# Moving split weights by 64 bytes in an encoder whose matmuls read them from SBUF

## The chip, the cores and the metric

The kernel runs on one core of one Trainium2 chip. The metric is the device time of one execution in microseconds (us); lower is better. All weights and activations are float32. TensorE multiplies in the reduced type float32r, and to keep more of the precision each operand is split into a high part ("hi", rounded to float32r) and a low part ("lo", the remainder).

## The reference

The reference is a two-layer encoder trunk on 256 tokens of width 2048. Layer 0 mixes tokens with a gated width-3 convolution, layer 1 with dilated banded attention (16 heads, three groups of dilation 1, 4 and 16). Each is followed by a gated feed-forward block of inner width 5632 with a width-3 convolution.

```
for i in range(2):
    h = rmsnorm(x, mix_norm_g[i])
    x = x + (short_conv_mixer if i == 0 else dilated_attention_mixer)(h, ...)
    h = rmsnorm(x, ffn_norm_g[i])
    x = x + conv_ffn(h, w_up[i], conv_w[i], conv_b[i], w_down[i])
return rmsnorm(x, final_norm_g)

short_conv_mixer: u, b, c = split(h @ w_in);  (b * dwconv3(c * u)) @ w_out
conv_ffn:         a, b = split(dwconv3(h @ w_up));  (silu(a) * b) @ w_down
attention:        softmax over |i-j| <= half within each dilation, groups joined by
                  their softmax denominators, then @ w_out
```

Nearly all the work is in the products with the weight matrices. All of them are read once from HBM.

## The kernel before

Activations lie transposed: 128 channels on the partitions, 16 blocks of channels, and for each block 256 tokens of hi followed by 256 tokens of lo (tiles `h`, `y`, `a`, `o`). A product with a 128x128 weight block takes two matmuls. The hi weights are loaded into TensorE, and 512 columns (hi and lo activations) stream past; then the lo weights are loaded, and the 256 columns of hi activations stream past. The product lo times lo is left out. Both add into one PSUM tile `ps`, whose halves are added on the way out (`gathered`: a ScalarE copy of one half, a VectorE addition of the other). Below, a "pair" is such a 512-column and 256-column matmul, and the load that runs during a stream is that of the next matmul.

Weights come through `load_w`: SyncE issues a DMA of up to 16 blocks into `raw` (four buffers), ScalarE rounds eight blocks at a time into the hi half of a `w2` tile, and VectorE subtracts to make the lo half. The four `w2` tiles are 8448 bytes per partition each, 33 times 256, and begin at multiples of 256 bytes. The hi blocks begin there; the lo blocks begin 4096 + 64 bytes further (`OFF = 16` words), so 64 bytes past a multiple of 256. Each block is 512 bytes wide, so this holds for every block. The activations `h`, `y`, `a`, `o` all begin at multiples of 256.

Four places use other forms. The first 16 blocks of each of the first three products come through `w2s`, whose hi and lo parts both begin at multiples of 256 (lines 205 to 210). The v projections of the attention (`v_unit`) swap the operands: blocks of `h` are the weights, all at multiples of 256, and a `w2v` tile (the `w2` buffers again) streams, beginning 64 bytes past a multiple; there the code issues eight 512-column matmuls, then eight 256-column ones. The last down-projection (`last`) uses three 256-column matmuls for each block, so that one VectorE addition ends a block. Scores, transposes and the product of probabilities and v are small and run between the q and k projections as tasks.

The order of instructions on each engine is set by the framework's scheduler out of the order of the code. In `mm` the code has eight hi matmuls, then eight lo matmuls of the same `w2` tile; the program that comes out of it alternates between them, 512 and 256 columns, wherever `mm` is used. The number of weight pairs that pass through `mm` (lines 108 and 110) is 6816; the v units have 768 (lines 374 and 377); the last down-projection has 176 blocks (lines 250 to 252).

Of the kernel before, what the change touches and what calls it, by code (L numbers as in the profile page):

```python
# [31 lines left out]
OFF = 16  # L32
W2 = 2 * 8 * P + 64
QSCALE = float(P) ** -0.5
# [3 lines left out]
def encoder_kernel(ctx: ExitStack, tc: tile.TileContext, xT, gs, scw, fcw, dist, w_first, w_in, w_so, w_v, w_qk, w_ao, w_up, w_dn, out):  # L38
# [42 lines left out]
    def load_w(src, n):  # L81
# [11 lines left out]
    def mm1(ps, w, a, start, stop):  # L93
        pe.matmul(ps, w[:, 0, :], a, start=start, stop=False)  # L94
        return pe.matmul(ps[:, :T], w[:, 1, :], a[:, :T], start=False, stop=stop)  # L95

    def mm(ps, parts, a, ks):


        n = len(parts)  # L100
        ks = list(ks)
        while ks:
            w2 = parts[ks[0]][0]
            now = [k for k in ks if parts[k][0] is w2]
            hi, lo = w2
            ks = ks[len(now) :]
            for k in now:
                pe.matmul(ps, hi[:, parts[k][1], :], a[:, k, :], start=k == 0, stop=False)  # L108
            for k in now:
                ins = pe.matmul(ps[:, :T], lo[:, parts[k][1], :], a[:, k, :T], start=False, stop=k == n - 1)  # L110
        return ins
# [66 lines left out]
    def add_to_x(ps, j):  # L178
        e = gathered(ps, "e0")
        dve.tensor_add(x[:, j, :], x[:, j, :], e)  # L180


    def short_conv():
        with tc.tile_pool(name="sc", bufs=1) as sp:
# [13 lines left out]
            for n in (1, 1, 2, 2, 3, 3, 2, 1, 1):  # L198
# [6 lines left out]
                w2 = sp.tile([P, 2, 3, 3 * P], F32R, name="w2s", tag="w2s", bufs=2)  # L205
                ins = split(w2[:, 0, :n, :], w2[:, 1, :n, :], raw[:, :n, :])
                for part in range(3):
                    for k in range(k0, k0 + n):
                        w = w2[:, :, k - k0, part * P : (part + 1) * P]
# [35 lines left out]
    def last(ps, parts, a, j):  # L245

        xj = x[:, j, :]
        for k in range(CH):
            (hi, lo), i = parts[k]
            pe.matmul(ps[:, :T], hi[:, i, :], a[:, k, T:], start=k == 0, stop=False)  # L250
            pe.matmul(ps[:, :T], lo[:, i, :], a[:, k, :T], start=False, stop=False)  # L251
            pe.matmul(ps[:, :T], hi[:, i, :], a[:, k, :T], start=False, stop=k == CH - 1)  # L252
        dve.tensor_add(xj, xj, ps[:, :T])
# [83 lines left out]
    def attention():  # L337
        with tc.tile_pool(name="att", bufs=1) as sp:
# [18 lines left out]
            def v_unit(hp, g):  # L357
# [239 lines left out]
```

## Time and profile before

| what | value |
|---|---|
| median of 3 runs | 2802.68 us (2802.38 to 2804.01) |
| profiled execution, its own time | 2801.87 us |
| its span, first to last instruction | 2800.1 us |
| granted TensorE clock, mean | 0.999 |
| PE (matmul) busy | 2783.2 us, 99% |
| PEld (weight load) busy | 2470.5 us, 88% |
| DVE (VectorE) busy | 1992.8 us, 71% |
| ACT (ScalarE) busy | 1504.0 us, 54% |
| HBM | 185 GB/s over the span |

The busy time of a matmul in the profile includes its way through the pipeline, so that consecutive ones overlap: the 512-column matmuls show 393 ns each and the 256-column ones 280 ns, though one follows the other sooner. What a matmul costs is the distance from its start to the next start. It is read from the timeline, from the pieces of the chain of waits (which are cut at the next start), or from the number of matmuls in a long stretch.

### The profile page before, as it was taken

Reading aid. Unit: us, or ns where it says so; the run is one execution under the profiler, and the core shown is the slowest. Engines: PE = TensorE matmul, PEld = TensorE weight load, DVE = VectorE, ACT = ScalarE, POOL = GpSimd, SP = SyncE. Lnnn points to the kernel's source line nnn. Section 1 sums busy time; section 2 is a strip of 40 time slices with the busy share of each in tenths; the row PEclk is TensorE's granted clock in tenths of the full one; section 3 lists DMA queues with packets and bytes.
Section 4 is the critical chain, followed back from the end, with each engine's and each line's share of the span. In section 5 each row is a group of like instructions: output and inputs, shape, how many; then the busy total and the mean of one; then the engine's idle time right before and its main releaser. Section 6 shows DMA issues by size and latency. Waiting matters only on the chain.

```text
span 2800.1 us, 40840 instructions
## 1 busy us (share of the span) xinstructions
PE 2783.2 (99%) x16388; PEld 2470.5 (88%) x16388; DVE 1992.8 (71%) x3065; ACT 1504.0 (54%) x2320; POOL 0.7 (0%) x6
## 2 busy tenths in 40 slices
PE   9999999999999999999999999999999999999998
PEld 7888888888888888888888888888888888888888
DVE  8777788876867768665665666666778876877865
ACT  6444566555655556544444444444565655555554
POOL 0000000000000000000000000000000000000000
PEclk9999999999999999999999999999999999999999
DMA  7555555546555456545445455455455546555553
GB/s 256 202 183 194 193 185 195 186 167 217 184 168 214 168 188 220 185 173 177 173 177 177 169 182 176 171 179 181 167 194 187 189 168 211 193 167 211 176 185 135
DMA packets 79822, 519.50 MB, mean 186 GB/s; under 512 B 9104, under 2 KB 10256, under 8 KB 28816
## 3 DMA queue, kind: packets, MB, share of 16 engines
q1 hardware_dynamic: 79488, 516.37, 52.4%
q8 instruction: 128, 2.10, 0.3%
q14 instruction: 62, 0.51, 0.1%
q10 hardware_dynamic: 144, 0.52, 0.0%
HBM read 514.76 MB, written 2.10 MB: 185 GB/s over the span
## 4 chain that ended last, share of the span: by engine, by line
PE 99%; DVE 0%; DMA 0%; SPq 0%; ACT 0%; issue 0%; DVEq 0%; ACTq 0%
PE ps L108 56%; PE ps L110 29%; PE ps L374 6%; PE ps L377 3%; PE ps L251 1%; PE ps L250 1%; PE ps L252 1%; PE ot L465 1%; PE s L423 1%; PE pt L442 1%; PE ot L460 0%; PE ps L94 0%; DMA raw<-in_w_first 0%; PE ps L95 0%; DVE x L284 0%; PE s L411 0%
## 5 line engine op out<-in xcount | busy, mean ns | idle before, releaser
L108 PE MATMUL ps<-h,w 128*128 128x512 f32 x5072 | 1769.0, 393 | 0.0
L110 PE MATMUL ps<-h,w 128*128 128x256 f32 x5072 | 1417.8, 280 | 0.0
L77 DVE TENSOR_TENSOR w<-raw,w 128x1024 fp32r<-128x1024 f32 (+1 forms) x954 | 1081.5, 1134 | 381.0 <-ACT w L76 362.2
L76 ACT CAST w<-raw 128x1024 fp32r<-128x1024 f32 (+1 forms) x954 | 934.0, 979 | 540.8 <-PE ps L110 423.8
L108 PEld LDWEIGHTS ps<-h,w 128*128 128x128 f32 x5072 | 952.2, 188 | 201.4
L110 PEld LDWEIGHTS ps<-h,w 128*128 128x128 f32 x5072 | 962.8, 190 | 0.5 <-DVE w L77 0.4
L120 ACT COPY tmp<-ps 128x256 f32<-128x256 f32 x464 | 172.3, 372 | 486.8 <-PE ps L110 486.8
L108 PE MATMUL ps<-a,w 128*128 128x512 f32 x1232 | 427.4, 392 | 0.0
L122 DVE TENSOR_TENSOR e<-ps,tmp 128x256 f32<-128x256 f32 x464 | 195.8, 422 | 243.9 <-ACT tmp L120 243.9
L110 PE MATMUL ps<-a,w 128*128 128x256 f32 x1232 | 344.3, 280 | 0.0
L108 PEld LDWEIGHTS ps<-a,w 128*128 128x128 f32 x1232 | 231.2, 188 | 49.4
L110 PEld LDWEIGHTS ps<-a,w 128*128 128x128 f32 x1232 | 233.9, 190 | 0.0
L374 PE MATMUL ps<-w2v,h 128*128 128x512 f32 x768 | 193.5, 394 | 0.0
L77 DVE TENSOR_TENSOR w2v<-rawv,w2v 128x1024 fp32r<-128x1024 f32 x96 | 117.6, 1225 | 98.1 <-ACT w2v L76 96.7
L374 PEld LDWEIGHTS ps<-w2v,h 128*128 128x128 f32 x768 | 137.6, 188 | 24.4
L76 ACT CAST w2v<-rawv 128x1024 fp32r<-128x1024 f32 x96 | 100.6, 1047 | 96.1 <-PE ps L377 69.4
L134 ACT ACTIVATE cv<-e,fcw_sb 128x256 f32<-128x256 f32 x176 | 105.8, 602 | 12.5 <-DVE e L129 11.9
L377 PEld LDWEIGHTS ps<-w2v,h 128*128 128x128 f32 x768 | 103.0, 188 | 8.0
L377 PE MATMUL ps<-w2v,h 128*128 128x256 f32 x768 | 105.0, 278 | 0.0
L129 DVE TENSOR_TENSOR e<-e,rr 128x256 f32<-128x256 f32 x220 | 93.0, 424 | 6.8
L135 DVE SCALAR_TENSOR_TENSOR cv<-e,fcw_sb,cv 128x255 f32<-128x255 f32 x176 | 84.1, 479 | 8.0 <-ACT cv L134 8.0
L136 DVE SCALAR_TENSOR_TENSOR cv<-e,fcw_sb,cv 128x255 f32<-128x255 f32 x176 | 85.1, 485 | 6.1
(120 smaller groups left out, 1711.6 us busy)
## 6 DMA issues: line engine op xcount, KB each, us to landing
raw<-in_w_up SPq DMA_DIRECT2D x176, 1024.0 KB, 4.8
raw<-in_w_qk SPq DMA_DIRECT2D x96, 1024.0 KB, 4.7
raw<-in_w_dn SPq DMA_DIRECT2D x128, 704.0 KB, 4.0
rawv<-in_w_v SPq DMA_DIRECT2D x48, 1024.0 KB, 5.0
raw<-in_w_in SPq DMA_DIRECT2D x45, 1024.0 KB, 4.8
raw<-in_w_so SPq DMA_DIRECT2D x16, 1024.0 KB, 4.8
raw<-in_w_ao SPq DMA_DIRECT2D x16, 1024.0 KB, 4.8
raw<-in_w_first SPq DMA_DIRECT2D x3, 384.0 KB, 5.6
```

Of the source, the lines that this page charges most:

```text
L76: ins = act.copy(hi, src)
L77: dve.tensor_sub(lo, src, f32(hi))
L108: pe.matmul(ps, hi[:, parts[k][1], :], a[:, k, :], start=k == 0, stop=False)
L110: ins = pe.matmul(ps[:, :T], lo[:, parts[k][1], :], a[:, k, :T], start=False, stop=k == n - 1)
L120: act.copy(tmp, ps[:, T:])
L122: dve.tensor_add(e, ps[:, :T], tmp)
L129: dve.tensor_mul(e, g, r)
L134: act.activation(c, e, AF.Identity, bias=w[:, 3:4], scale=w[:, 1:2])
L135: dve.scalar_tensor_tensor(c[:, 1:], e[:, : T - 1], w[:, 0:1], c[:, 1:], op0=ALU.mult, op1=ALU.add)
L136: dve.scalar_tensor_tensor(c[:, : T - 1], e[:, 1:], w[:, 2:3], c[:, : T - 1], op0=ALU.mult, op1=ALU.add)
L374: pe.matmul(ps[i], h[:, k, i * P : (i + 1) * P], w2[:, k - k1, :, :], start=k == 0, stop=False)
L377: pe.matmul(ps[i][:, :T], h[:, k, T + i * P : T + (i + 1) * P], w2[:, k - k1, 0, :], start=False, stop=k == KT - 1,)
```

## The change

Offsets are given in words of 4 bytes. In the `w2` tiles the hi blocks now begin at word 16 (64 bytes past a multiple of 256) and the lo blocks at word 1088 (a multiple of 256); the same is done to `w2s`. For the v units the `w2v` tile is laid out as four lo blocks from word 0 and four hi blocks from word 1040 (64 bytes past a multiple), and the 512-column stream takes the lo block first and then the hi block, by a stride. The 256-column stream is the hi block. The v units, `mm` and all but the last block row of the last down-projection (15 of 16) are written as 512 and 256 columns in turn; in the last down-projection these 15 now use `mm` and `add_to_x`, which is a ScalarE copy and two VectorE additions in place of one VectorE addition.

```diff
-OFF = 16
 W2 = 2 * 8 * P + 64
+HI = 16
+LO = 8 * P + 64
+LOV = 0
+LOS = 9 * P + 64
+HIV = 4 * 2 * P + 16
...
-            hi, lo = (w2[:, z : z + 8 * P].rearrange("p (k c) -> p k c", k=8) for z in (0, 8 * P + OFF))
+            hi, lo = (w2[:, z : z + 8 * P].rearrange("p (k c) -> p k c", k=8) for z in (HI, LO))
...
     def mm(ps, parts, a, ks):
         n = len(parts)
-        ks = list(ks)
-        while ks:
-            w2 = parts[ks[0]][0]
-            now = [k for k in ks if parts[k][0] is w2]
-            hi, lo = w2
-            ks = ks[len(now) :]
-            for k in now:
-                pe.matmul(ps, hi[:, parts[k][1], :], a[:, k, :], start=k == 0, stop=False)
-            for k in now:
-                ins = pe.matmul(ps[:, :T], lo[:, parts[k][1], :], a[:, k, :T], start=False, stop=k == n - 1)
+        for k in ks:
+            (hi, lo), i = parts[k]
+            pe.matmul(ps, hi[:, i, :], a[:, k, :], start=k == 0, stop=False)
+            ins = pe.matmul(ps[:, :T], lo[:, i, :], a[:, k, :T], start=False, stop=k == n - 1)
         return ins
...
-                w2 = sp.tile([P, 2, 3, 3 * P], F32R, name="w2s", tag="w2s", bufs=2)
-                ins = split(w2[:, 0, :n, :], w2[:, 1, :n, :], raw[:, :n, :])
+                w2 = sp.tile([P, LOS + 9 * P], F32R, name="w2s", tag="w2s", bufs=2)
+                w2 = [w2[:, z : z + 9 * P].rearrange("p (k c) -> p k c", k=3) for z in (HI, LOS)]
+                ins = split(w2[0][:, :n, :], w2[1][:, :n, :], raw[:, :n, :])
...
     def last(ps, parts, a, j):
-        for k in range(CH):
-            (hi, lo), i = parts[k]
-            pe.matmul(ps[:, :T], hi[:, i, :], a[:, k, T:], start=k == 0, stop=False)
-            pe.matmul(ps[:, :T], lo[:, i, :], a[:, k, :T], start=False, stop=False)
-            pe.matmul(ps[:, :T], hi[:, i, :], a[:, k, :T], start=False, stop=k == CH - 1)
-        dve.tensor_add(xj, xj, ps[:, :T])
+        if j < KT - 1:
+            mm(ps, parts, a, range(CH))
+            add_to_x(ps, j)
+        else:
...
-                        w2 = w2[:, OFF : OFF + 8 * T].rearrange("p (k z c) -> p k z c", k=4, z=2)
-                        split(w2[:, :, 0, :], w2[:, :, 1, :], raw[:, k1 - k0 : k1 - k0 + 4, :])
+                        lo, hi = (w2[:, z : z + 4 * T].rearrange("p (k c) -> p k c", k=4) for z in (LOV, HIV))
+                        split(hi, lo, raw[:, k1 - k0 : k1 - k0 + 4, :])
+                        both = w2[:, : 2 * HIV].rearrange("p (z c) -> p z c", z=2)
                         for k in range(k1, k1 + 4):
+                            c = (k - k1) * T
                             for i in range(2):
-                                pe.matmul(ps[i], h[:, k, i * P : (i + 1) * P], w2[:, k - k1, :, :], start=k == 0, stop=False)
-                        for k in range(k1, k1 + 4):
-                            for i in range(2):
+                                pe.matmul(ps[i], h[:, k, i * P : (i + 1) * P], both[:, :, c : c + T], start=k == 0, stop=False)
                                 pe.matmul(
-                                    ps[i][:, :T], h[:, k, T + i * P : T + (i + 1) * P], w2[:, k - k1, 0, :],
+                                    ps[i][:, T:], h[:, k, T + i * P : T + (i + 1) * P], hi[:, k - k1, :],
                                     start=False, stop=k == KT - 1,
                                 )
```

Where `mm` was used before, TensorE's order stays as it was. It changes in two places. The first is the entry into the attention's v units on TensorE; the rows name the line, the operation, the tile written and those read, and the columns that stream. Before:

```order
L108 MATMUL ps<-a,w_10305 128x512
L110 MATMUL ps<-a,w_10305 128x256
L374 MATMUL ps<-w2v,h 128x512 x8
L377 MATMUL ps<-w2v,h 128x256 x8
L374 MATMUL ps<-w2v,h 128x512 x8
```

After:

```order
L108 MATMUL ps<-a,w_10305 128x512
L109 MATMUL ps<-a,w_10305 128x256
L380 MATMUL ps<-w2v,h 128x512
L381 MATMUL ps<-w2v,h 128x256
L380 MATMUL ps<-w2v,h 128x512
```

The same matmuls in number and size, now one of 512 columns, one of 256.

The second place is the last down-projection, here one block row on ScalarE (L76 and L81 make hi weights, L153 and L152 square the sum, L256 and L260 multiply by the norm's gain). Before:

```order
L76 CAST w_25763<-raw 128x1024
L76 CAST w_25766<-raw 128x384
L153 ACTIVATE sq<-x 128x256
L256 ACTIVATE x<-x,g_sb 128x256
L76 CAST w_25810<-raw 128x1024
```

After:

```order
L119 COPY tmp<-ps 128x256
L81 CAST w_25766<-raw 128x384
L152 ACTIVATE sq<-x 128x256
L81 CAST w_25806<-raw 128x1024
L260 ACTIVATE x<-x,g_sb 128x256
```

One copy out of PSUM is added for each block row. On TensorE each of these 15 block rows has 22 matmuls (11 pairs) where it had 33 of 256 columns; the last block row keeps its 33, and with it the end of the program is as it was.

More of the change, by code (lines that the diff above doesn't have):

```diff
@@ L247, in last @@
         xj = x[:, j, :]
-        for k in range(CH):
-            (hi, lo), i = parts[k]
-            pe.matmul(ps[:, :T], hi[:, i, :], a[:, k, T:], start=k == 0, stop=False)
-            pe.matmul(ps[:, :T], lo[:, i, :], a[:, k, :T], start=False, stop=False)
-            pe.matmul(ps[:, :T], hi[:, i, :], a[:, k, :T], start=False, stop=k == CH - 1)
-        dve.tensor_add(xj, xj, ps[:, :T])
+        if j < KT - 1:
+            mm(ps, parts, a, range(CH))
+            add_to_x(ps, j)
+        else:
+            for k in range(CH):
+                (hi, lo), i = parts[k]
+                pe.matmul(ps[:, :T], hi[:, i, :], a[:, k, T:], start=k == 0, stop=False)
+                pe.matmul(ps[:, :T], lo[:, i, :], a[:, k, :T], start=False, stop=False)
+                pe.matmul(ps[:, :T], hi[:, i, :], a[:, k, :T], start=False, stop=k == CH - 1)
+            dve.tensor_add(xj, xj, ps[:, :T])
         if j < KT - 1:
@@ L384, in v_unit @@
                     tmp = tp.tile([P, T], F32, name="tmp", tag="tmp")
-                    act.mul(tmp, ps[i][:, T:], rc[:, i : i + 1])
+                    act.mul(tmp, ps[i][:, :T], rc[:, i : i + 1])
                     e = tp.tile([P, T], F32, name="e", tag="e0") if g == 0 else v[:, i, :]
-                    dve.scalar_tensor_tensor(e, ps[i][:, :T], rc[:, i : i + 1], tmp, op0=ALU.mult, op1=ALU.add)
+                    dve.scalar_tensor_tensor(e, ps[i][:, T:], rc[:, i : i + 1], tmp, op0=ALU.mult, op1=ALU.add)
                     if g == 0:
```

6 lines of the change are left out of this document (3 added, 3 removed).

## The prediction

> **What bounds the kernel now.** I read the page first: engines, slices, chain, groups.
>
> ```profile
> PE 2783.2 (99%) x16388; PEld 2470.5 (88%) x16388; DVE 1992.8 (71%) x3065; ACT 1504.0 (54%) x2320; POOL 0.7 (0%) x6
> PEclk9999999999999999999999999999999999999999
> PE 99%; DVE 0%; DMA 0%; SPq 0%; ACT 0%; issue 0%; DVEq 0%; ACTq 0%
> L108 PE MATMUL ps<-h,w 128*128 128x512 f32 x5072 | 1769.0, 393 | 0.0
> L110 PE MATMUL ps<-h,w 128*128 128x256 f32 x5072 | 1417.8, 280 | 0.0
> ```
>
> TensorE sets the time from start to end: it is 99% of the chain, its matmuls wait for nothing (the last column is 0.0 idle), and the granted clock is at the top in all slices. So only the distance between matmuls counts. The count of matmuls in a stretch gives it, and the timeline gives its two parts.
>
> ```profile
> 300.00:800.00 500.00, 499.80 (x1442) 270.52 (x1441) 1.00 0.53 186
> ...
> 1200.40 0.28 PE L110 MATMUL ps<-h,w 128*128 128x256 f32 x1
> 1200.40 0.19 PEld L108 LDWEIGHTS ps<-h,w 128*128 128x128 f32 x1
> 1200.51 0.39 PE L108 MATMUL ps<-h,w 128*128 128x512 f32 x1
> 1200.52 0.19 PEld L110 LDWEIGHTS ps<-h,w 128*128 128x128 f32 x1
> 1200.74 0.28 PE L110 MATMUL ps<-h,w 128*128 128x256 f32 x1
> ```
>
> The first row is line 108 alone: 1442 matmuls in 500 us, so a pair takes 500 / 1442 = 346.7 ns. In the timeline the 512-column stream takes 0.23 us (1200.51 to 1200.74), and the 256-column one the rest, about 117 ns. Each load begins with the stream before its own. So during a 512-column stream the lo weights are read (64 past a multiple, the stream itself at a multiple), and during a 256-column stream the hi weights (both at a multiple). 6816 pairs at 346.7 ns are 2363 us of the 2800.
>
> **Does the address matter at all?** The v units answer best, in the chain of waits, whose pieces (start, length, what) end at the next start:
>
> ```profile
> 1323.81 1.84 PE ps L374 x8
> 1325.65 0.94 PE ps L377 x8
> 1326.60 1.83 PE ps L374 x8
> 1328.43 0.91 PE ps L377 x8
> 1329.34 1.83 PE ps L374 x8
> 1331.17 0.94 PE ps L377 x8
> 1332.11 1.83 PE ps L374 x8
> 1333.94 0.91 PE ps L377 x8
> 1334.85 0.44 PE s L423 x4
> ```
>
> Here all streams begin 64 past a multiple and all loads at one. The 512-column stream takes 1.83 / 8 = 228.8 ns. The 256-column stream has two steady lengths, 0.94 / 8 = 117.5 and 0.91 / 8 = 113.8 ns, with the same instructions and addresses; each holds for a run of eight. From 1323.81 to 1334.85 are 32 pairs, so 345.0 ns a pair. The startup has a third arrangement, everything at a multiple, and alternates like the main loop:
>
> ```profile
> 22.48 0.23 PE ps L94
> 22.71 0.12 PE ps L95
> 22.83 0.23 PE ps L94
> 23.06 0.11 PE ps L95
> 23.17 0.23 PE ps L94
> ...
> 25.25 0.23 PE ps L94
> 25.49 0.12 PE ps L95
> 25.60 0.23 PE ps L108
> ```
>
> Nine pairs from 22.48 to 25.60 are 3.12 us, 346.7 ns each; the 256-column streams take 0.11 and 0.12 in turn, about 115, which leaves 231.7 ns for the 512-column ones. The last down-projection has 256-column streams alone, all at a multiple; the loads during L251 and L252 are at a multiple, that during L250 (the lo weights of L251) 64 past one:
>
> ```profile
> 2753.06 0.28 PE L250 MATMUL ps<-a,w 128*128 128x256 f32 x1
> 2753.17 0.28 PE L251 MATMUL ps<-a,w 128*128 128x256 f32 x1
> 2753.29 0.28 PE L252 MATMUL ps<-a,w 128*128 128x256 f32 x1
> ...
> 2755.18 0.28 PE L250 MATMUL ps<-a,w 128*128 128x256 f32 x1
> ...
> L250 PEld LDWEIGHTS ps<-a,w 128*128 128x128 f32 x176 | 33.1, 188 | 0.0
> L251 PEld LDWEIGHTS ps<-a,w 128*128 128x128 f32 x176 | 33.8, 192 | 0.0
> ```
>
> Six blocks from 2753.06 to 2755.18 are 2.12 us, 353.3 ns for three, 117.8 each. The load at 64 past takes 192 ns instead of 188, and its stream is no longer than the others. So stream and load do act on each other, by a few ns, and the same pair of addresses can settle at more than one length.
>
> **The change part by part.** *Addresses in the main loop.* Afterwards the lo weights, at a multiple like the stream, are read during the 512-column stream, and the hi weights, 64 away from the stream, during the 256-column one. For the 256-column stream the nearest rows with a difference of 64 are the v units' (113.8 or 117.5) and L250's (117.8). For the 512-column stream with no difference there is the startup alone (231.7); with a difference, 228.8 in the v units. Bounds of the pair: at best 228.8 + 112 (a little below 113.8, as the startup's 0.11 allows) = 340.8; at worst 231.7 + 117.8 = 349.5. I take the v units' short length for the 256-column stream, because a difference of 64 is what separates them from the main loop, which stays at 117, and for the 512-column stream the middle of its two rows, 230.3. That makes 344.1 ns, 2.6 less than 346.7, times 6816: 17.7 us less.
>
> *v units.* 768 pairs go from 345.0 to 344.1 if they behave as the main loop does: 0.7 us less. With bounds of 340.8 and 349.5 it is 3.2 less to 3.5 more.
>
> *Last down-projection.* 15 x 11 = 165 blocks go from 353.3 to 344.1: 1.5 us less (bounds 2.1 and 0.6 less). What it adds is cheap:
>
> ```profile
> L120 ACT COPY tmp<-ps 128x256 f32<-128x256 f32 x464 | 172.3, 372 | 486.8 <-PE ps L110 486.8
> L122 DVE TENSOR_TENSOR e<-ps,tmp 128x256 f32<-128x256 f32 x464 | 195.8, 422 | 243.9 <-ACT tmp L120 243.9
> ```
>
> 372 ns on ScalarE and another 422 ns on VectorE for each block row lie beside some 3.8 us of TensorE work (11 pairs at 344). Uncovered they would cost 15 x 0.8 = 12 us; both engines idle in front of these very operations waiting for TensorE, so I take nothing. The last block row, behind which nothing could hide, keeps its old form.
>
> *Order in* `mm` *and startup.* The executed order there already alternates, so the rewritten loop moves nothing. The 48 startup pairs are worth 48 x 2.6 ns = 0.1 us.
>
> *Cover.* A faster TensorE asks for weights 0.8% sooner: 186 GB/s in the row above, at a DMA share of 0.53, becomes 187.4. VectorE at 71% and ScalarE at 54% have room.
>
> Sum: 17.7 + 0.7 + 1.5 + 0.1 = 20 us less than the profiled execution's 2801.9, 2781.9; the runs' median lies 0.8 above that execution, so 2783.
>
> A rule speaks against any effect. The Trainium skill, "TensorE: Matmul & The Clock Gate", section "Step-by-step: what each phase is for", says that the streaming operand and the weight load have independent SBUF read ports, so that loading the next weights takes nothing from the running matmul. By it the addresses are indifferent and only the new order in the last down-projection would count. Its section "Back-to-back issue gap" gives N / 2.4 + 2.5 ns, so 215.8 and 109.2, an estimate of 325 ns for a pair; the trace disagrees with 346.7, and the two lengths in the v units speak for some interaction, so I lean away from the rule without excluding it.
>
> **The rivals.**
>
> *The pair time stays.* For it: two arrangements that alternate 512 and 256, the main loop's and the startup's, differ in their addresses and both come to 346.7; what one stream gained the other lost (231.7 + 115 against 230 + 117). If a third arrangement does so too, the v units lose 768 x 1.7 ns = 1.3 us, the last down-projection gains 165 x 6.6 = 1.1, and the time is 2803. Against it: nothing in the startup has a difference of 64 under the short stream. This is also where the page's rule of separate ports ends.
>
> *The short stream is held by its load, and the time goes up.* The 256-column stream is the one that has hardly longer than its load needs. With the load at 64 past a multiple the load takes 192 ns in place of 188, and the only alternating rows for the long stream at equal addresses say 231.7. Then the pair is the upper bound, 349.5, and the sum 6816 x 2.8 = 19.1, plus 3.5 for the v units, less 0.6: 22 us more, 2825. It decides once 117.8 and 231.7 come together, above 346.7 in sum. Against it: L250's own stream was no longer for the longer load, and in the startup the 231.7 went with 115.
>
> *The larger gain.* Both streams settle at their shortest, 340.8: 6816 x 5.9 = 40.2, plus 3.2 and 2.1, 45 us less, 2757. Nothing in the trace shows both at once.
>
> **How the numbers follow.** My forecast of a pair at 342 to 346 has 0.42, the larger gain 0.10, no change 0.25, the slower rival 0.23. About 0.2% (5.6 us, 0.8 ns a pair) is what a measurement of this kernel can tell from no change. Faster thus has 0.52, same 0.25, slower 0.23. The likeliest gives 2783, and its own range is 2771 (228.8 + 113.8 = 342.6 a pair, 31 us less) to 2796. For 8 in 10 the range must reach to the other signs: 2756 to 2820, which leaves out the upper end of the slower rival and a little below.
>
> **What would show it.** In the same 500 us window line 108 should count 500 / 0.3441 = 1453 matmuls in place of 1442; 1442 means no change, 1431 the slower rival. In the timeline the 256-column starts should be followed by the next within 114 ns, and the 512-column ones within about 230; the hi loads should read near 192 ns, the lo loads 188, the reverse of now. The v units should show the same pair time as the main loop; if they gain and the main loop does not, the order was worth more than the address. A block row of the last down-projection should take 3.8 us in place of 3.9. The forecast is wrong if the short stream stays at 117 or if the long one pays back what it gains; a wait of TensorE for `w2` or `ps` would mean that the cover was thinner than the idle times say.

## The result: one kernel, four times

The changed kernel ran 16 times. The executions don't scatter round one value; they fall into four groups:

| executions | time, us |
|---|---|
| 3 | 2770.87 to 2771.07 |
| 3 | 2793.92 to 2794.43 |
| 1 | 2801.36 |
| 9 | 2823.35 to 2825.70 |

The median of all 16 is 2823.44 us. The kernel before, run 16 times beside it, gave 2802.8 (2801.5 to 2804.0) in one group. The ratio to before, 0.9937 (95% interval 0.9912 to 0.9963), is taken over the seven executions up to 2801 alone, since executions more than 1.5% above the fastest count as slow; the other nine, at the same granted clock, turn out to belong to the change itself. So by that ratio the kernel is 0.6% faster; by the median of all executions it is 0.7% slower. No execution came near the 2783 that was forecast.

The profiled execution is one of the first group, 2770.87 us with a span of 2768.8. Its page, engines, clock, chain and groups (operation, count, busy time, mean ns, idle before):

```profile
PE 2750.9 (99%) x16223; PEld 2432.0 (88%) x16223; DVE 1995.9 (72%) x3080; ACT 1502.1 (54%) x2335; POOL 0.7 (0%) x6
PEclk9999999999999999999999999999999999999999
PE 99%; DMA 1%; DVE 0%; ACT 0%; SPq 0%; issue 0%; DVEq 0%; ACTq 0%
L108 PE MATMUL ps<-h,w 128*128 128x512 f32 x5072 | 1748.6, 392 | 0.3 <-ACT w L81 0.3
L109 PE MATMUL ps<-h,w 128*128 128x256 f32 x5072 | 1406.8, 277 | 0.0
L119 ACT COPY tmp<-ps 128x256 f32<-128x256 f32 x479 | 177.5, 371 | 471.1 <-PE ps L109 471.1
L121 DVE TENSOR_TENSOR e<-ps,tmp 128x256 f32<-128x256 f32 x479 | 201.9, 422 | 228.4 <-ACT tmp L119 228.4
```

TensorE is still 99% of the chain at the full clock, and waits for next to nothing (0.3 us of idle before line 108). The 15 added copies and additions (479 in place of 464) cost nothing: both engines still idle for TensorE in front of them.

A second profile of the same kernel, unchanged, was taken later and fell into the largest group (2825.15 us, span 2823.0):

```profile
PE 2804.7 (99%) x16223; PEld 2467.7 (87%) x16223; DVE 1998.4 (71%) x3080; ACT 1505.3 (53%) x2335; POOL 0.7 (0%) x6
PE 99%; DMA 1%; DVE 0%; ACT 0%; SPq 0%; issue 0%; DVEq 0%; ACTq 0%
L108 PE MATMUL ps<-h,w 128*128 128x512 f32 x5072 | 1782.5, 395 | 0.8 <-ACT w L81 0.8
L109 PE MATMUL ps<-h,w 128*128 128x256 f32 x5072 | 1423.8, 281 | 0.0
```

Same instructions, same chain, no new wait (0.8 us against 0.3), and 54 us more. The mean matmul has become 3 and 4 ns longer, the 512-column one 395 for 392, the 256-column one 281 for 277. The view of windows says where. It counts the 512-column matmuls of `mm` in 800 us of the first feed-forward block and 400 us of the second (columns: stretch, length, TensorE busy and count, weight load busy and count, clock, DMA share, GB/s). Before, then the changed kernel's 2771 us execution, then its 2825 us one:

```profile
100.00:900.00 800.00, 799.80 (x2307) 432.93 (x2307) 1.00 0.54 190
2060.00:2460.00 400.00, 400.00 (x1155) 216.51 (x1154) 1.00 0.54 189
```

```profile
100.00:900.00 800.00, 799.80 (x2352) 441.34 (x2352) 1.00 0.55 194
2060.00:2460.00 400.00, 400.00 (x1177) 220.76 (x1177) 1.00 0.54 190
```

```profile
100.00:900.00 800.00, 799.80 (x2286) 429.12 (x2285) 1.00 0.53 188
2060.00:2460.00 400.00, 399.80 (x1143) 214.39 (x1143) 1.00 0.53 187
```

800 / 2307 is 346.8 ns a pair before. Afterwards it is 800 / 2352 = 340.1 in one execution and 800 / 2286 = 350.0 in the other, over hundreds of us without a break, and never the 344.1 of the forecast. The clock column is 1.00 in all six rows. In the timeline (start, length in us, engine, line, operation) the 2771 us execution at 800 us, and the 2825 us one:

```profile
800.06 0.39 PE L108 MATMUL ps<-a,w 128*128 128x512 f32 x1
800.29 0.28 PE L109 MATMUL ps<-a,w 128*128 128x256 f32 x1
800.40 0.39 PE L108 MATMUL ps<-a,w 128*128 128x512 f32 x1
```

```profile
800.09 0.40 PE L108 MATMUL ps<-h,w 128*128 128x512 f32 x1
800.32 0.28 PE L109 MATMUL ps<-h,w 128*128 128x256 f32 x1
800.44 0.39 PE L108 MATMUL ps<-h,w 128*128 128x512 f32 x1
```

800.06 to 800.40 against 800.09 to 800.44. From the trace's start times, which have more digits, the streams take 227 + 113 ns in the short form and 231 to 233 + 118 in the long one. Both streams are longer, not one of them.

**Where the four groups come from.** Cutting the trace at every place where the alternation of 512 and 256 columns breaks, and taking the mean pair of each piece, gives two long stretches: 2974 pairs up to the attention (in the 2771 us execution from 67 us to 1079) and 2314 behind it (from 1964 us on). Each keeps one length throughout in both profiles; the small matmul of the norm inside each (at 366 and 2042 us) does not change it. If a stretch is at 350 in place of 340, it costs 2974 x 10 ns = 29.7 us or 2314 x 10 ns = 23.1 us. From 2771 that makes 2771, 2794, 2801 and 2824: the four groups. The pairs with both stretches at 340 and with both at 350 have a profile of this kernel; the two middle groups have only the sum (and the kernel with the new address alone, below, which shows the mixed case).

In the 2771 us profile 5544 pairs of `mm` ran at 340 ns and 1357 near 350, nearly all of the latter in the attention, where small matmuls break the stream every 15 to 48 pairs. Against before that is 5544 x 6.7 ns = 37.1 us less and 1357 x 3.3 = 4.5 us more.

**The v units** lost. In the chain of waits of the 2771 us execution (start, length, what):

```profile
1208.73 0.23 PE ps L380
1209.08 0.23 PE ps L380
1209.42 0.23 PE ps L380
1209.65 0.12 PE ps L381
1209.77 0.25 PE ps L380
...
1215.70 0.23 PE ps L380
```

The view lists the longer pieces only, so most of the short streams (L381) are left out. 20 pairs from 1208.73 to 1215.70 are 6.97 us, 348.5 each, and some 512-column streams take 0.25 us (at 1209.77). All 24 v units together took 269.6 us in place of 267.4.

**The last down-projection** gained. The timeline at its middle:

```profile
2721.87 0.39 PE L108 MATMUL ps<-a,w 128*128 128x512 f32 x1
...
2725.61 0.39 PE L108 MATMUL ps<-a,w 128*128 128x512 f32 x1
```

Eleven pairs are a block row: 3.74 us, in place of 3.89.

Working back: 37.1 - 4.5 - 2.2 (v units) is 30.4 us less, and 1.1 more for the last down-projection, whose blocks took 353.3 rather than the 346.7 assumed in that count (165 x 6.6 ns). That is 31.5; measured between the two profiled executions are 31.0.

### The profile page after: what moved, and what is told of

It reads as the page before. It is cut to its first block, busy times and chain, and to the rows that moved or that the text cites. A ratio compares the mean times of both kernels' runs of the same rounds, so it can differ in the third digit from the quotient of the medians.

```text
span 2768.8 us, 40538 instructions
## 1 busy us (share of the span) xinstructions
PE 2750.9 (99%) x16223; PEld 2432.0 (88%) x16223; DVE 1995.9 (72%) x3080; ACT 1502.1 (54%) x2335; POOL 0.7 (0%) x6
## 4 chain that ended last, share of the span: by engine, by line
PE 99%; DMA 1%; DVE 0%; ACT 0%; SPq 0%; issue 0%; DVEq 0%; ACTq 0%
PE ps L108 57%; PE ps L109 29%; PE ps L380 6%; PE ps L381 3%; PE ot L469 1%; PE s L427 1%; PE pt L446 1%; PE ot L464 0%; DMA raw<-in_w_first 0%; DMA raw<-in_w_in 0%; DVE x L288 0%; PE s L415 0%; PE s L413 0%; PE s L414 0%; DVE w2s L82 0%; PE stat L169 0%
## 5 line engine op out<-in xcount | busy, mean ns | idle before, releaser
L108 PE MATMUL ps<-h,w 128*128 128x512 f32 x5072 | 1748.6, 392 | 0.3 <-ACT w L81 0.3
L81 ACT CAST w<-raw 128x1024 fp32r<-128x1024 f32 (+1 forms) x954 | 934.7, 980 | 523.9 <-PE ps L109 420.4
L108 PE MATMUL ps<-a,w 128*128 128x512 f32 x1397 | 475.3, 389 | 0.0
L109 PE MATMUL ps<-a,w 128*128 128x256 f32 x1397 | 385.6, 276 | 0.0
L121 DVE TENSOR_TENSOR e<-ps,tmp 128x256 f32<-128x256 f32 x479 | 201.9, 422 | 228.4 <-ACT tmp L119 228.4
L108 PEld LDWEIGHTS ps<-a,w 128*128 128x128 f32 x1397 | 262.2, 188 | 54.5
L380 PE MATMUL ps<-w2v,h 128*128 128x512 f32 x768 | 270.4, 396 | 0.0
L109 PEld LDWEIGHTS ps<-a,w 128*128 128x128 f32 x1397 | 262.2, 188 | 0.0
L381 PE MATMUL ps<-w2v,h 128*128 128x256 f32 x768 | 213.3, 278 | 0.0
L82 DVE TENSOR_TENSOR w2v<-rawv,w2v 128x1024 fp32r<-128x1024 f32 x96 | 117.5, 1224 | 99.8 <-ACT w2v L81 99.0
L380 PEld LDWEIGHTS ps<-w2v,h 128*128 128x128 f32 x768 | 144.1, 188 | 33.6
L81 ACT CAST w2v<-rawv 128x1024 fp32r<-128x1024 f32 x96 | 100.6, 1048 | 98.2 <-PE ps L381 69.8
L381 PEld LDWEIGHTS ps<-w2v,h 128*128 128x128 f32 x768 | 144.3, 188 | 0.0
```

Source lines behind the costliest of these rows:

```text
L81: ins = act.copy(hi, src)
L82: dve.tensor_sub(lo, src, f32(hi))
L108: pe.matmul(ps, hi[:, i, :], a[:, k, :], start=k == 0, stop=False)
L109: ins = pe.matmul(ps[:, :T], lo[:, i, :], a[:, k, :T], start=False, stop=k == n - 1)
L121: dve.tensor_add(e, ps[:, :T], tmp)
L380: pe.matmul(ps[i], h[:, k, i * P : (i + 1) * P], both[:, :, c : c + T], start=k == 0, stop=False)
```

## The experiments

The question was why one set of addresses gives two lengths, what chooses, and whether the change's gain can be had without the loss. The theories at the start: the address alone sets one length (the prediction's), the address allows two lengths and something at the start of a stretch chooses (settling), and the separate ports of the Trainium skill, "TensorE: Matmul & The Clock Gate", section "Step-by-step: what each phase is for" (no effect of the address; something outside TensorE makes the difference).

### Every address, with nothing else running

TensorE alone runs 16 x 8 stretches of 32 pairs. Hi and lo weights begin 0, 64, 128 or 192 bytes past a multiple of 256, the streams at a multiple, and a different small matmul leads each stretch. Behind the first stretch, which is left out, there is no DMA, ScalarE or VectorE work meanwhile.

```diff
+    ADDRESSES = [(i, j) for i in range(4) for j in range(4)]
+    for zh, zl in ADDRESSES:
+        hi, lo = wz[0, zh], wz[1, zl]
+        for r in range(8):
...
+            for k in range(32):
+                pe.matmul(ps, hi[:, k % 8, :], h[:, k % KT, :], start=k == 0, stop=False)
+                pe.matmul(ps[:, :T], lo[:, k % 8, :], h[:, k % KT, :T], start=False, stop=k == 31)
```

> A measuring kernel that leaves the encoder out: weights and activations are loaded once, then TensorE alone runs 128 stretches of 32 pairs (512 columns over hi weights, 256 over lo weights, all streams at a multiple of 256 bytes). The hi and the lo weights each begin 0, 64, 128 or 192 bytes past a multiple, 16 combinations, and ahead of each of a combination's eight stretches stands another small matmul (a float32 one of 128 columns, three of 256 columns, one of 128 to 168 columns in steps of 8). Theory of settling: a stretch takes one of a few lengths of the pair, set by the addresses, and which of them is set by the small matmul in front; at (64, 0) both 340 and 350 ns appear, at (0, 64) and (0, 0) 346.7 alone. Theory of one length for each address: every combination shows one length whatever stands in front, and what differs between the changed kernel's stretches comes from ScalarE, VectorE or DMA, which are idle here. Theory of separate ports: all 16 combinations show the same length.

Measured, ns for a pair over the steady part of each stretch, out of the trace's start times (first column: hi offset, first row: lo offset):

| | lo 0 | lo 64 | lo 128 | lo 192 |
|---|---|---|---|---|
| hi 0 | 346.6 or 353.3 | 346.7 | 346.7 (two at 350) | 346.7 to 351 |
| hi 64 | 340.0 (4 of 8) or 350.0 (4) | 353.3 | 350 or 353.3 | 353.3 |
| hi 128 | 352.0 | 346.6 | 351 | 346.7 or 353.3 |
| hi 192 | 340.0 (5 of 8) or 350.0 (3) | 346.7 or 353.3 | 346.7 | 349 to 353.3 |

The arrangement before (hi 0, lo 64) gives 346.7 in all eight stretches. The one after (64, 0) gives two lengths, and so, unlike expected, does (0, 0). Two stretches side by side in the timeline, the same addresses, the second behind another small matmul:

```profile
389.69 0.39 PE L86 MATMUL ps<-h,w 128*128 128x512 f32 x1
...
399.14 0.40 PE L86 MATMUL ps<-h,w 128*128 128x512 f32 x1
...
402.69 0.39 PE L86 MATMUL ps<-h,w 128*128 128x512 f32 x1
...
410.85 0.39 PE L86 MATMUL ps<-h,w 128*128 128x512 f32 x1
```

27 pairs in 9.45 us are 350.0 ns; 24 pairs in 8.16 us are 340.0. So the choice is TensorE's own: no other engine and no transfer runs there. The rule of the Trainium skill that the prediction weighed ("TensorE: Matmul & The Clock Gate", "Step-by-step: what each phase is for") is not borne out by these matmuls: by it alone the 16 arrangements would agree, and they run from 340.0 to 353.3 ns with everything else idle. Whether a load gives way to a stream or a stream to a load is not shown; the streams' own address was not varied.

### The address alone, and the order alone

Two edits of the kernel before. The first moves only the `w2` tiles that `mm` reads; v units, startup and last down-projection keep their old form:

```diff
-            hi, lo = (w2[:, z : z + 8 * P].rearrange("p (k c) -> p k c", k=8) for z in (0, 8 * P + OFF))
+            hi, lo = (w2[:, z : z + 8 * P].rearrange("p (k c) -> p k c", k=8) for z in (16, 8 * P + 64))
```

> The kernel before with the new offsets of the w2 tiles alone; v units, last down-projection and w2s as before. Theory of settling: the same lengths of the pair as in the changed kernel, 340 or 350 ns, held over hundreds of us, so execution times in groups near 2771, 2794, 2801 and 2824 us, each within 3 us of the changed kernel's. If the new order is what matters: 2802 us and 346.7 ns a pair as before.

Of 12 executions nine lie between 2801.35 and 2802.43, one at 2793.41, two at 2822.64 and 2825.09: three of the four groups expected, and none at 2771; the median is 2801.85, the ratio 1.001 (0.9991 to 1.0029). The windows of its profiled execution (2802.31 us):

```profile
100.00:900.00 800.00, 799.80 (x2285) 429.12 (x2285) 1.00 0.53 188
2060.00:2460.00 400.00, 399.80 (x1176) 220.55 (x1176) 1.00 0.55 195
```

The first stretch is at 350, the second at 340, in one execution. That it comes out as the kernel before did is a cancellation: 2315 pairs of `mm` at 340 are 15.5 us less (6.7 ns each), and 4421 at 350 are 14.6 us more (3.3 each). A median that says "no change" hides a gain and a loss of 15 us. The address alone thus makes the split; and which length is taken differs between this kernel and the changed one, though the long stretches hold the same instructions.

The second edit keeps the old addresses and takes only the order: v units in turn, last down-projection through `mm`.

```diff
                         for k in range(k1, k1 + 4):
                             for i in range(2):
                                 pe.matmul(ps[i], h[:, k, i * P : (i + 1) * P], w2[:, k - k1, :, :], start=k == 0, stop=False)
-                        for k in range(k1, k1 + 4):
-                            for i in range(2):
                                 pe.matmul(
...
+        if j < KT - 1:
+            mm(ps, parts, a, range(CH))
+            add_to_x(ps, j)
```

> The kernel before with the new order alone: v units and the last down-projection alternate 512 and 256 columns, all weights stay where they were (hi at a multiple of 256, lo 64 past). Theory of settling: main loop at 346.7 ns as before, the last down-projection 15 x 11 x 6.6 ns = 1.1 us shorter, the v units within 2 us: 2800 to 2804 us, in one group. If the order is what matters: about 2771 us in some executions.

Measured: ten executions in one group, 2804.6 to 2806.8, median 2806.2, ratio 1.0013 (1.0004 to 1.0022). Everywhere in `mm` the pair is 346.7. The v units took 271.5 us, 4.1 more than in eights. So the order in the v units is a loss at the old addresses, somewhat larger than expected, and the four groups don't come from the order.

### What chooses between 340 and 350

TensorE alone again: at (64, 0) and at (192, 0) a first stretch, then one of 14 beginnings, then the pairs, each beginning four times behind different first stretches. A beginning is a small matmul of n columns, several of 256 columns, or another order of the first pairs ("hhll" is 512, 512, 256, 256).

```diff
+    BEGINS = [32, 64, 96, 128, 160, 192, 256, (256, 256), (256, 256, 256), "hhll", "hhhlll", "hhhhllll", "hllh", "hhlhll"]
+    for zh, zl in ((1, 0), (3, 0)):
+        for begin in BEGINS:
+            for before in (128, 136, 160, 168):
+                small(before)
+                stretch(hi, lo, "hl" * 16)
...
```

> The measuring kernel again (the encoder left out, TensorE alone), hi weights 64 or 192 bytes past a multiple of 256, lo weights at one. 112 times: a small matmul of 128, 136, 160 or 168 columns, 16 pairs (which settle at 340 or 350 ns), then a disturbance, then 22 to 24 pairs. Disturbances: one matmul of 32 to 256 columns, two or three of 256, or only another order of the first matmuls (two of 512 and then two of 256, three and three, four and four, and others). Theory of settling by phase: what is set after a disturbance follows from the disturbance (and perhaps from the length before), the same each time; at least one disturbance ends at 340 ns from all four beginnings, so that the kernel can be made to settle there. Rival, settling by chance: each disturbance ends at 340 in about half of the cases, without a pattern, and no way to steer it.

Measured, at (192, 0): behind a small matmul of 32 to 160 columns the pairs go to 340 from either length; behind one of 192 from 340 to 350; one or two of 256 keep what was there, three of them give 340; every change of order gives 340 from either length. A beginning hhll costs some 34 ns once where the pairs are at 340 already. At (64, 0) hhll is as clear, with 350 from either in all four, and one of 96 columns keeps what was there. Most other beginnings have no such pattern there: 32 columns give 340 twice and 350 twice, hhhlll from 340 gives 340 once and 350 once, and three beginnings lead in some cases to a third length, 353. So at (192, 0) the length isn't thrown by chance; it follows from what stands at the start of a stretch, and then holds. At (64, 0) the beginning and the length before it do not always settle the outcome, and what else enters was not found. (192, 0) is the better of the two.

Finer steps of address were tried in the same form, 32 bytes apart, 64 combinations:

```diff
-        for z in range(4):
+        for z in range(8):
...
-            t = wz[part, z][:, 16 * z : 16 * z + 8 * P].rearrange("p (k c) -> p k c", k=8)
+            t = wz[part, z][:, 8 * z : 8 * z + 8 * P].rearrange("p (k c) -> p k c", k=8)
```

> The measuring kernel with hi and lo weights at each of 0, 32, 64 to 224 bytes past a multiple of 256, 64 combinations, three stretches of 20 pairs each, streams at a multiple. If 64-byte steps are what counts: 32 past goes like 0 or like 64, and no combination lies below 340 ns. If finer steps count: some combination away from the multiples of 64 lies below 340 ns, towards 330, or shows 340 in all three stretches where (64, 0) shows 350 in some.

340 appears at (64, 0) and (192, 0) alone, and nothing lies below it. Offsets that are no multiple of 64 gave 346 to 354, but for one stretch at 343 (96, 32) and one at 344 (224, 0).

### The choice forced in the whole kernel

If the start of a stretch chooses, the same beginning in front of each product should put all executions into one group: hhll at 64 all at 350, hhll at 192 all at 340. Three kernels, run together: the changed kernel with every product begun hhll; the same with the hi weights at 192; and the hi weights at 192 with nothing else.

```diff
-        for k in ks:
-            (hi, lo), i = parts[k]
...
+        steps = [(part, k) for k in ks for part in range(2)]
+        steps[1:3] = steps[2:0:-1]
```

> The changed kernel (hi 64 past, lo at a multiple) in which each product through mm begins with two matmuls of 512 columns and then two of 256, and alternates after that. In the measuring kernel this beginning led to 350 ns at these addresses from either length. Theory of settling by phase: all products run at 350 ns, 6981 pairs x 350 = 2443 us, plus 33 ns for each of 485 beginnings, 16 us, and everything else as in the changed kernel's profile, some 376 us: 2835 us in one group, with nothing near 2771 or 2794. Rival, chance or something outside TensorE: the groups at 2771, 2794, 2801 and 2824 stay, each a few us later.

```diff
-HI = 16
+HI = 48
...
+        steps = [(part, k) for k in ks for part in range(2)]
+        steps[1:3] = steps[2:0:-1]
```

> The same beginning with the hi weights 192 past a multiple (lo at one), where the measuring kernel went to 340 ns from either length. Theory of settling by phase: 6981 pairs x 340 = 2373.5 us, plus 34 ns for each of 485 beginnings, 16.5 us, and the other 376 us: 2766 us in one group. Rival, chance: several groups between 2771 and 2840 us.

```diff
-HI = 16
+HI = 48
```

> The changed kernel with one number changed, the hi weights 192 instead of 64 bytes past a multiple; no special beginnings. Theory of settling by phase: the attention's products, which follow small matmuls of 128 or 256 columns, settle at 340 ns more often than in the changed kernel (there mostly 350), some 8 us less; the long stretches follow a wait for a DMA and settle at 340 or at 350, so groups remain: about 2762, 2785, 2792 and 2815 us. Rival, the address alone: one group.

Their windows, in this order (the 512-column line):

```profile
100.00:900.00 800.00, 789.09 (x2288) 419.98 (x2287) 1.00 0.53 188
2060.00:2460.00 400.00, 394.50 (x1144) 209.97 (x1143) 1.00 0.53 188
```

```profile
100.00:900.00 800.00, 789.37 (x2338) 427.00 (x2337) 1.00 0.54 192
2060.00:2460.00 400.00, 394.72 (x1170) 213.47 (x1169) 1.00 0.53 189
```

```profile
100.00:900.00 800.00, 799.80 (x2353) 441.52 (x2352) 1.00 0.55 194
2060.00:2460.00 400.00, 400.00 (x1178) 220.91 (x1177) 1.00 0.54 189
```

| kernel | executions, us | ratio to before (95%) | pairs |
|---|---|---|---|
| hi at 64, hhll | 2822.1 to 2823.4, median 2822.84 | 1.0071 (1.0056 to 1.0086) | 320 of 342 units of 16 pairs at 350 |
| hi at 192, hhll | 2771.6 to 2773.4, median 2772.77 | 0.9894 (0.9877 to 0.991) | all but one of these units at 340 |
| hi at 192 | 2760.7 to 2765.0, median 2762.46 | 0.9857 (0.9842 to 0.9872) | 6630 pairs at 340, 272 at 350 |

Four executions of each, one group each. At 64 the beginning hhll left the largest of the four groups alone. Four times the largest is not much by itself, since nine of 16 executions fell there without it; but in the profile nearly every product, begun anew, runs at 350. For hi at 192 the third kernel weakens the test: without any special beginning it came out in one group too, as its rival expected (the address alone) and not as the theory did (groups up to 2815 us). So that the long stretches run at 340 in the second kernel can be the work of the address as well as of the beginning. What hhll does at 192 shows in the attention, where 272 pairs are at 350 without it. With TensorE alone the beginning leads to 350 at 64 and to 340 at 192; the kernels agree with it in both directions, the second one in these pairs only.

Two sizes were missed. At 350 the beginning costs nothing (2288 pairs in 800 us, against 2286 in the 2825 us execution without it), so the first of the three came at 2823 where 2835 was expected. At 340 it costs what was expected: 2338 pairs in 800 us against 2353 without it are 15 x 340 ns = 5.1 us for 156 beginnings, 33 ns each. The 7 us by which the second came above 2766 lie elsewhere: the sum priced every pair at 340.0, and the pairs beside small matmuls and waits take longer; in the profile of hi at 192 alone such extras come to some 8 us. Forcing at each product is dearer than leaving it, and hi at 192 alone does best of the three. A later repeat of that kernel on another chip gave 2760.5 to 2763.8, median 2762.08, ratio 0.9856:

> The kernel with hi at 192 once more, to see whether more executions show groups. If the wait for a DMA at the start can still send a long stretch to 350 ns, some executions lie 23 to 53 us above 2762. If what follows at these addresses leads to 340 from most phases, all lie between 2760 and 2766.

All four lie in the narrow range. But its profile (2763.84 us) has the attention's out-projection, 230 pairs, at 350, and 340 behind the norm's small matmul. So at 192, too, the second long stretch can start at 350; the norm then ended it.

The second profile of the changed kernel, shown above beside the result, was taken for the same question, whether its largest group differs in a wait or only in the length:

> The changed kernel once more, for its trace. Theory of settling: the time follows from the lengths of its two long stretches alone, 2974 pairs in the first half and 2314 in the second: 2771 us with both at 340 ns, 2794 with the second at 350, 2801 with the first at 350, 2824 with both. Rival: the trace shows other waits or a lower clock in the longer executions.

It differs only in the length: 350 in both long stretches, no other wait, the same clock.

The two profiles also show the moment of the choice in the first long stretch. TensorE catches up with the weights, and two 512-column matmuls and later two 256-column ones follow each other. The timeline of the 2771 us execution, with one weight load (PEld) that waits:

```profile
64.45 0.19 PEld L109 LDWEIGHTS ps<-h,w 128*128 128x128 f32 x1 [0.24 <-DVE w L82]
...
66.44 0.40 PE L108 MATMUL ps<-h,w 128*128 128x512 f32 x1
...
66.79 0.40 PE L108 MATMUL ps<-h,w 128*128 128x512 f32 x1
67.03 0.40 PE L109 MATMUL ps<-h,w 128*128 128x256 f32 x2
67.26 0.39 PE L108 MATMUL ps<-h,w 128*128 128x512 f32 x1
...
67.60 0.39 PE L108 MATMUL ps<-h,w 128*128 128x512 f32 x1
```

and of the 2825 us one:

```profile
65.07 0.19 PEld L109 LDWEIGHTS ps<-h,w 128*128 128x128 f32 x1 [0.25 <-DVE w L82]
...
67.01 0.39 PE L108 MATMUL ps<-h,w 128*128 128x512 f32 x1
...
67.35 0.39 PE L108 MATMUL ps<-h,w 128*128 128x512 f32 x1
67.58 0.40 PE L109 MATMUL ps<-h,w 128*128 128x256 f32 x2
67.81 0.40 PE L108 MATMUL ps<-h,w 128*128 128x512 f32 x1
...
68.16 0.39 PE L108 MATMUL ps<-h,w 128*128 128x512 f32 x1
```

The two 256-column matmuls in a row (the row with x2) lead from 353 ns a pair (the mean from 65.38 to 66.79) to 340 in the one, and from 340 to 350 in the other. The two executions part some 2 us earlier. Until 64 us both run at 350. Then a load of lo weights waits for VectorE's subtraction (the first row of each); VectorE works without a gap there, 11.00 of the 11 us from 55 to 66 in both. Behind the wait the one goes on at 353, the other at 340. By the start times the delayed 256-column matmul takes 195 ns in the one and 199 in the other. So a small difference at one wait, some 65 us into the program, goes with a difference that lasts a thousand us. It is a wait for VectorE and not for a DMA, which the expectations above had named. It gives no rule yet: in the profile of the kernel with the new address alone the same place has 203 ns, then 353 a pair, and behind the two 256-column matmuls 350 and not 340. What makes the executions differ there was not varied by itself. The second long stretch, entered behind the attention, also begins after two 256-column matmuls in a row; why it differs between executions is open.

### Is there a version that beats both?

From hi at 192 two further steps. First: the v units in their old layout and order, and hhll in front of the few products that still ran at 350, those behind the product of probabilities and v, and the one behind the first norm (17 in all).

```diff
+        if settle:
+            steps[1:3] = steps[2:0:-1]
...
-                    ins = mm(ps, w, h, range(KT))
+                    ins = mm(ps, w, h, range(KT), j == 1 and part == 2)
...
-                mm(ps, w, h, range(KT))
+                mm(ps, w, h, range(KT), heads.pop("settle", False))
```

> The kernel with hi at 192 and lo at a multiple, with the v units in their old layout and order (267.4 us in the profile before, 269.6 in the changed kernel's), and with the beginning 512, 512, 256, 256 at only 17 products: those behind the probability-times-v task and one behind the first norm, which still ran at 350 ns. Theory of settling: 272 pairs go from 350 to 340 (2.7 us), 17 x 34 ns are added (0.6), the v units give back 2: some 2758 us in one group. Rival: another order somewhere shifts the phase of the products that follow, and groups up to 2815 us come back.

Five of six executions lie between 2757.29 and 2758.93, one at 2780.06; the median is 2758.56, the ratio 0.9858 (0.9835 to 0.9881). The v units are back at 267.3 us. The one at 2780 is near the price of a second long stretch at 350 (23.1 us), as the rival had it; it was not profiled. The profile of the 2757.29 one has 230 pairs, the attention's out-projection, at 350, which the norm then turned to 340.

So the second step puts hhll also at the first products of each part of the feed-forward blocks and at one of the out-projection, so that no long stretch depends on what comes before.

```diff
-                        mm(ps, w, h, range(KT))
+                        mm(ps, w, h, range(KT), i == 0)
...
-                    mm(ps, w, a, range(CH))
+                    mm(ps, w, a, range(CH), j == 0)
...
-                    mm(ps, w, o, range(KT))
+                    mm(ps, w, o, range(KT), j == 2)
```

> The e8 kernel, one of whose six executions lay 22 us above the others (about 2314 pairs at 10 ns, the second long stretch), with the beginning 512, 512, 256, 256 added at the first products of each up- and down-projection part and at the third of the attention's output projection. Theory of settling: each long stretch is now led to 340 ns wherever it starts; 230 pairs of the output projection gain 2.3 us, some 23 beginnings cost 34 ns each, 0.8 us: 2757 us, and no execution near 2780. Rival: the 2780 had another cause, and comes back in about one of six.

```profile
100.00:900.00 800.00, 799.13 (x2352) 440.57 (x2351) 1.00 0.55 194
2060.00:2460.00 400.00, 399.60 (x1177) 220.27 (x1176) 1.00 0.54 190
```

Five executions in one group, 2757.45 to 2759.86, median 2758.63, ratio 0.9844 (0.983 to 0.9857). It is 44 us faster than before and 12 faster than the best group of the changed kernel. Five executions without an outlier don't prove that there is none: the first step had one in six.

## Why the prediction was right or wrong

*TensorE's matmul distance is all that counts, and the address of the weights moves it.* Right. TensorE is 99% of the chain in both profiles, and with all other engines idle the address still changes the pair by up to 13.3 ns.

*One pair length after the change, 344.1 ns: the 256-column stream at 113.8, the 512-column one in the middle of its two rows, 230.3.* This is the step that failed. The 256-column stream does reach 113 ns, and then the 512-column one takes 227, less than the shorter row; or they take 118 and 231 to 233. In the long stretches the pair is 340.0 or 350.0, and the middle does not occur. The two ends that were taken as bounds, 340.8 and 349.5, were within a ns of what occurs, but as two outcomes of one kernel and not as an uncertainty about one value. The hint stood in the prediction: the v units' 256-column stream "has two steady lengths, 0.94 / 8 = 117.5 and 0.91 / 8 = 113.8 ns, with the same instructions and addresses; each holds for a run of eight", and "the same pair of addresses can settle at more than one length". What should have followed is a forecast of groups: with the long stretches known from the program, 340.8 and 349.5 in each of two stretches. Instead one of the two lengths was picked for the short stream and a mean for the long one, and the mean of two states is a value that no run shows.

*The rivals "the larger gain" (2757) and "the short stream is held by its load" (2825).* Both times were nearly met, in different executions: the fastest group is 14 us above the first, because the attention stayed mostly at 350, and the largest group is within 2 us of the second. The second's mechanism was wrong: it has the short stream held by a load of 192 ns from 64 past a multiple. The hi loads, now at 64 past, take 429.12 us / 2285 = 187.8 ns in the 2825 us execution (the 800 us row above), against 441.34 / 2352 = 187.6 in the other. It is the lo loads, now at a multiple, that become longer there, while both streams are longer. Line 109 in the same 800 us, the 2771 us execution and then the 2825 us one (length, matmuls busy and count, loads busy and count):

```profile
100.00:900.00 800.00, 649.04 (x2353) 441.35 (x2352) 1.00 0.55 194
100.00:900.00 800.00, 641.97 (x2285) 433.76 (x2285) 1.00 0.53 188
```

441.35 / 2352 is 187.6 ns and 433.76 / 2285 is 189.8. In the 2825 us execution half of the lo loads in this stretch read 192 ns, in the other none does. So the load of 192 ns goes with the longer pair here and not with the 64 bytes; the prediction expected it at the hi loads.

*The pair time stays (2803).* It did not. The median of the kernel with the new address alone, 2801.85, looks like it, but there 350 in one stretch pays for 340 in the other.

*Line 108 counts 1453 in 500 us.* By the 800 us rows it is 1470 in the one execution and 1429 in the other.

*v units, 0.7 us less.* Wrong sign: 2.2 us more. The term took the change to be worth what it is worth in the main loop. The order costs 4.1 us by itself at the old addresses (271.5 against 267.4), and the new layout gives back 1.9. The pair there is 348.5 ns and not the main loop's 340 or 350.

*Last down-projection, 1.5 us less, 3.8 us a block row.* 15 x 0.147 = 2.2 us less at 3.740 us, since its pairs were at 340 in the profiled execution; at 350 the row would be 3.85 and the gain 0.5, so both bounds given are about the two lengths. The added copies are hidden, as the sum had it.

*Order in `mm` unchanged, weights arrive in time.* Right: 194 GB/s at a DMA share of 0.55, and no wait for `w2` or `ps` worth a us.

*The sum.* 2783 with 2756 to 2820. By the ratio (0.9937) the direction is right, and even the size: 0.9937 x 2802.8 is 2785. That is luck, the mean of three executions at 2771, three at 2794 and one at 2801, none of them near it. By the median of all executions the direction is wrong, and nine of 16 lie a few us above the range. The chances (0.52 faster, 0.23 slower) had both signs, but as alternatives between kernels, not between executions of one.

## What to carry to other kernels

Where a profile shows one instruction with the same operands at two steady lengths, don't average them and don't choose one: price each by the stretch for which it would hold, and reckon with executions that fall into groups at the sums. Look at all executions before a ratio or a median, since a median of "no change" may be a gain and a loss of 10 ns a pair in different stretches. And when two lengths exist, look for an address or a beginning that always leads to the short one; here moving the hi weights by a further 128 bytes turned 2771 to 2826 us into 2761 to 2765.

## What was not expected of the hardware

- TensorE alone, with weights 64 or 192 bytes past a multiple of 256 for one load and at one for the other, runs the same alternating matmuls at 340.0 or 350.0 ns a pair. The length is set at the start of an unbroken stretch and holds for as long as it lasts, here up to some 1000 us; a single small matmul of the norm did not end it at 64, but turned 350 into 340 in two profiles at 192.
- 64 and 192 bytes differ. At 192 every change of order led to 340, at 64 hhll led to 350 in the experiment with TensorE alone and in the kernel, and other beginnings led now to one length, now to another. The prediction had thought of a distance from a multiple as all that counts; no rule that covers the 16 offsets was found.
- Many of the steady lengths met are 340.0, 346.7, 350.0 and 353.3 ns, multiples of 3.33 ns; 348.9, 351.1 and 352.0 also occur and are none. What sets these values was not tried.
